# A decoder layer's last stage: seven block products in place of eight, over pairs of 512-token chunks

## The chip, the core and the metric

The kernel runs on one core of a Trainium2 chip. The metric is the device time of one execution in microseconds (us); lower is better. The engines of the core run their own instruction streams side by side: TensorE (PE, matrix products; PEld is its loading of the stationary operand), VectorE (DVE), ScalarE (ACT), GpSimd (POOL) and SyncE (SP, which here issues all transfers). An engine takes its instructions strictly in order and waits at one whose inputs or buffers aren't ready. PE writes its results to PSUM banks, from which DVE and ACT read them; everything else on chip lies in SBUF, 128 partitions wide.

## The reference

One layer for 2048 tokens of width 1024, float32. The stage that changes computes, for a hidden state h that is a scaled and shifted x:

```
u, B, C, g_conv, m_attn, m_conv = h @ W_in columns          (each 1024 wide)
a = (o * silu(g_attn)) @ W_attn_out                         (512 -> 1024)
z = C * u;  y_conv = causal 3-tap convolution of z along tokens + bias
s = (B * y_conv * silu(g_conv)) @ W_conv_out                (1024 -> 1024)
y = (sigmoid(m_attn) * a + sigmoid(m_conv) * s) @ W_o       (1024 -> 1024)
out = LayerNorm(alpha * x + (1 + gate) * y)
```

Ahead of it stands the attention: three dilated groups of heads whose outputs are merged per head with weights from their softmax denominators, and gated, which gives o * silu(g_attn).

## The kernel before

To keep float32 accuracy each operand of a product is split into a rounded high part and the remainder (`split`, L99 and L100: a cast on ACT, then a subtraction on DVE), and a product is three matmuls, high x high, high x low, low x high (L137 to L139). A matmul takes a stationary tile of 128x128 and a moving tile of 128x512.

Stage 1 does two of the attention groups, stage 1b the local group and the merge, stage 2 all the rest. The merge of a head (L561 to L574) loads the weights broadcast from `al_scr` into `ab`, the other groups' outputs into `og`, multiplies and adds on DVE, and stores the result into `om_scr`.

The work of all stages is a list of segments run by `run_segs` (L162): a segment has a weight tile `raw` of 128x1024, whose load is issued five segments ahead and whose split is issued three ahead, and a function that issues its matmuls and what consumes them. Because the list runs across stages and chunks, the preparation of the next chunk and the last merges of stage 1b are issued between matmuls of other work. The order on each engine is then the scheduler's, which sorts by priority in the order of the code and by its estimate of when things are ready.

Stage 2 (L592 to L818) goes through four chunks of 512 tokens. For each chunk it has the eight 128-row tiles of h split (`hhi`, `hlo`), and then, for each of eight column blocks of 128, the projections u, C, g_conv, B (24 matmuls each), with the convolution and the gates on DVE and ACT between them; then for each of eight blocks the two mixes m_attn and m_conv (24 each), the attention output (12) and the convolution output (24), merged into `mg` and split; then the w_o products, token blocks stationary (192 matmuls), and the normalization. One chunk has 1632 matmuls. Nothing of a chunk goes to DRAM but the result. The gate row of the normalization is computed with dots on DVE (L233) during the mixes of the first chunk. The first products of a chunk have the weights stationary and h moving, those with w_o have the merged tokens (`mgh`, `mgl`) stationary and the weights moving (names `hhi`, `whi`).

## Time and profile before

| what | value |
|---|---|
| time, median of three runs | 2704.84 us (2702.08 to 2707.76) |
| the profiled execution's span | 2700.4 us |
| PE busy | 2646.0 us, 98% |
| DVE, ACT, POOL busy | 50%, 32%, 2% |
| moved by DMA | 325.00 MB, mean 120 GB/s |

A row of busy time counts an instruction of an engine from start to end; matmuls overlap each other, so their single durations (some 390 ns) are longer than the distance between two of them. A row of a timeline is the start in us, the duration in us, the engine, the line, the operation and the tiles written and read; what stands in brackets is idle time ahead of it and what ended it. A "granted clock" is the share of PE's full clock that the throttle let it have.

### The profile page before, as it was taken

To read this page: it belongs to the slowest core of one execution; us is meant where nothing else is said; L and a number is where in the kernel's file an instruction comes from. 1 tells how busy PE (TensorE), PEld (TensorE's weight loads), DVE (VectorE), ACT (ScalarE), POOL (GpSimd) and SP (SyncE) were. 2 spreads that over 40 slices of the span, in tenths; PEclk is the share of its full clock that TensorE was granted. 3 is DMA by queue.
4 is the path that set the end of the run, shared out by engine and by line. 5 is a ranking of instruction groups with operands and counts; after the bars stand their busy time and mean duration, and the time that the engine had idled before them with its cause. 6 is when DMAs were issued, how large, how long until landed. Compare 5 with 4: busy or idle time off the path is not lost.

```text
span 2700.4 us, 32783 instructions
## 1 busy us (share of the span) xinstructions
PE 2646.0 (98%) x12910; PEld 2257.3 (84%) x12910; DVE 1346.5 (50%) x2330; ACT 870.3 (32%) x1471; POOL 55.0 (2%) x78
## 2 busy tenths in 40 slices
PE   6999999999999999999999999999999999999998
PEld 4898998989988888887888888888888888888887
DVE  8334334243245765857454564433654434644336
ACT  4233333233333434433232323322232323233221
POOL 2000000000000000000000000000000000000000
PEclk9999999999999999999999999999999999999999
DMA  7223223232233544626233442322432323423222
GB/s 260 82 79 125 82 95 109 75 113 87 74 126 106 186 146 129 204 97 220 102 125 123 147 159 94 113 94 97 160 129 94 117 91 112 163 95 107 96 98 101
DMA packets 141357, 325.00 MB, mean 120 GB/s; under 512 B 18215, under 2 KB 53107, under 8 KB 141204
## 3 DMA queue, kind: packets, MB, share of 16 engines
q1 hardware_dynamic: 141204, 322.92, 35.8%
q8 instruction: 101, 1.65, 0.2%
q14 instruction: 52, 0.43, 0.1%
HBM read 301.58 MB, written 21.28 MB: 120 GB/s over the span
## 4 chain that ended last, share of the span: by engine, by line
PE 88%; DVE 5%; DMA 5%; issue 1%; ACT 0%; SPq 0%; DVEq 0%
PE mm L137 22%; PE mm L138 22%; PE mm L139 22%; PE mm L185 4%; PE mm L184 3%; PE mm L183 3%; DMA og<-o_scr 1%; PE pt L364 1%; DMA xs<-in_xn 1%; DMA ab<-al_scr 1%; DVE hlo L100 1%; PE mm L785 1%; PE mm L783 1%; PE mm L784 1%; PE s L184 1%
## 5 line engine op out<-in xcount | busy, mean ns | idle before, releaser
L137 PE MATMUL mm<-hhi,whi 128*128 128x512 f32 x2392 | 940.3, 393 | 22.2 <-ACT hhi L99 21.4
L138 PE MATMUL mm<-hlo,whi 128*128 128x512 f32 x2392 | 934.1, 391 | 2.2 <-DVE hlo L100 2.2
L139 PE MATMUL mm<-hhi,wlo 128*128 128x512 f32 x2392 | 933.8, 390 | 0.7 <-DVE wlo L100 0.7
L100 DVE TENSOR_TENSOR wlo<-raw,whi 128x1024 fp32r<-128x1024 f32 x423 | 517.4, 1223 | 827.5 <-ACT whi L99 817.5
L99 ACT CAST whi<-raw 128x1024 fp32r<-128x1024 f32 x423 | 444.4, 1051 | 1370.6 <-PE mm L138 598.6
L137 PEld LDWEIGHTS mm<-hhi,whi 128*128 128x128 f32 x2392 | 450.1, 188 | 115.5 <-ACT hhi L99 24.2
L139 PEld LDWEIGHTS mm<-hhi,wlo 128*128 128x128 f32 x2392 | 450.0, 188 | 95.2 <-DVE wlo L100 1.6
L138 PEld LDWEIGHTS mm<-hlo,whi 128*128 128x128 f32 x2392 | 450.4, 188 | 94.4 <-DVE hlo L100 4.1
L183 PE MATMUL mm<-whi,hhi 128*128 128x256 f32 x768 | 246.2, 322 | 3.8 <-ACT hhi L99 3.6
L185 PE MATMUL mm<-whi,hlo 128*128 128x256 f32 x768 | 245.1, 323 | 1.3 <-DVE hlo L100 1.1
L184 PE MATMUL mm<-wlo,hhi 128*128 128x256 f32 x768 | 244.8, 321 | 1.0 <-DVE wlo L100 1.0
L183 PEld LDWEIGHTS mm<-whi,hhi 128*128 128x128 f32 x768 | 182.2, 237 | 7.9 <-ACT hhi L99 6.4
L185 PEld LDWEIGHTS mm<-whi,hlo 128*128 128x128 f32 x768 | 181.4, 237 | 3.9 <-DVE hlo L100 3.2
L184 PEld LDWEIGHTS mm<-wlo,hhi 128*128 128x128 f32 x768 | 181.8, 237 | 1.9 <-DVE wlo L100 1.2
L357 ACT ACTIVATE p<-p,st 128x128 f32<-128x128 f32 (+1 forms) x192 | 86.7, 453 | 71.3 <-DVE st L355 70.8
L137 PE MATMUL mm<-cph,whi 128*128 128x512 f32 x256 | 100.6, 393 | 0.0
L139 PE MATMUL mm<-cph,wlo 128*128 128x512 f32 x256 | 100.2, 392 | 0.0
L138 PE MATMUL mm<-cpl,whi 128*128 128x512 f32 x256 | 99.7, 390 | 0.0
L729 DVE TENSOR_TENSOR sc<-sc,mm 128x512 f32<-128x512 f32 x32 | 22.0, 688 | 123.0 <-PE mm L139 123.0
L99 ACT CAST hhi<-xs 128x512 fp32r<-128x512 f32 x96 | 58.1, 619 | 76.9 <-DVE xs L122 65.4
L122 DVE TENSOR_SCALAR xs<-xs,scp,mod 128x512 f32<-128x512 f32 x96 | 51.4, 543 | 41.0 <-DMA xs<-in_xn 25.4
L100 DVE TENSOR_TENSOR hlo<-xs,hhi 128x512 fp32r<-128x512 f32 x96 | 66.2, 705 | 5.3 <-ACT hhi L99 4.6
(210 smaller groups left out, 2632.0 us busy)
## 6 DMA issues: line engine op xcount, KB each, us to landing
raw<-in_w_main SPq DMA_DIRECT2D x304, 512.0 KB
raw<-in_w_v SPq DMA_DIRECT2D x48, 512.0 KB
xs<-in_xn SPq DMA_DIRECT2D x64, 256.0 KB
raw<-in_w_co SPq DMA_DIRECT2D x32, 512.0 KB
raw<-in_w_o SPq DMA_DIRECT2D x32, 512.0 KB
ab<-al_scr SPq DMA_DIRECT2D x48, 256.0 KB
...
```

The lines of the kernel that those rows point to most:

```text
L99: S.copy(hi, src)
L100: V.tensor_sub(lo, src, hi.bitcast(F32))
L122: E.tensor_scalar(xs, xs, scp[:, k:k + 1], mod[:, 0, k:k + 1], op0=ALU.mult, op1=ALU.add)
L137: PE.matmul(ps, hi[:, sl], xh, start=k == 0, stop=False)
L138: PE.matmul(ps, hi[:, sl], xl, start=False, stop=False)
L139: PE.matmul(ps, lo[:, sl], xh, start=False, stop=k == n - 1)
L183: PE.matmul(o, a[0], b[0], start=start, stop=False)
L184: PE.matmul(o, a[0], b[1], start=False, stop=False)
L185: PE.matmul(o, a[1], b[0], start=False, stop=stop)
L357: S.activation(pt[:, w], pt[:, w], AF.Exp, scale=-1.0, bias=st[:, 0, col:col + 1], accum_out=st[:, 1, col:col + 1])
L364: PE.transpose(ps[:, n * P:(n + 1) * P], P_t[b][:, a:a + P], ident)
L783: PE.matmul(ps, xh[:, ts], hi, start=k == 0, stop=False)
```

## The change

Stage 2 is written anew for two pairs of chunks (1024 tokens each) and in four parts, A to D, each run to its end over all tokens before the next begins. A product of a 2x2 grid of weight blocks and a 2x2 grid of activation blocks takes eight block products; the changed kernel forms seven, from sums and differences of blocks (the Winograd form of Strassen's scheme).

- `t_row` builds for one 128-row of the moving operand the seven combinations: four subtractions and seven splits, into tiles `th` and `tl` of their own for each product and row, one buffer each. For parts A to C the moving operand is h, the gated attention, the gated convolution; for D it is w_o, scaled by the gate row first.
- `stationary_parts` builds for each step the seven combinations of the stationary operand: four sums, three 1024-wide splits (`w2`) and one 512-wide (`w1`).
- `products` issues the seven products in the order 1, 2, 6, 5, 7, 4, 3 into four banks a to d. A bank is copied by ACT (`keep`) and then accumulated onto by the next product; DVE adds a copy and a bank to get each of the four result blocks. `step` issues the loads and stationary parts of a step, and only then (`flush`) the products of the step before.
- Between the parts results go to DRAM and back: `y_scr` (gated convolution), `sg_scr` (the mixes), `pa_scr` (attention output times its mix), `mg_scr` (merged), 42 MB in all.
- The dots of the gate row move from the mixes to part B. In part C, POOL adds the two merged halves, and in part D it adds the LayerNorm's bias; both were on DVE.
- Pools for weights, h and PSUM are now closed with stage 1b, and stage 2 has its own.
- In part D rows are handled 1024 wide, with the normalization on ACT (`Identity` with scale and bias).

```diff
+    y_scr = dram.tile([2, KT, P, 2 * CH], F32, name="y_scr")
+    sg_scr = dram.tile([2, 2, KT, P, 2 * CH], F32, name="sg_scr")
+    pa_scr = dram.tile([2, KT, P, 2 * CH], F32, name="pa_scr")
+    mg_scr = dram.tile([SEQ // P, P, KT, P], F32, name="mg_scr")
...
+    tp = ctx.enter_context(tc.tile_pool(name="tp", bufs=1, reuse_waits="tile"))
+    psum = ctx.enter_context(tc.tile_pool(name="psum2", bufs=1, space=bass.MemoryType.PSUM, reuse_waits="tile"))
...
+    def t_split(T, p, i, src):
+        hi = tp.tile([P, CH], F32R, name=f"th{p}{i}")
+        lo = tp.tile([P, CH], F32R, name=f"tl{p}{i}")
+        split(hi, lo, src)
+        T[p, i] = (hi, lo)
...
+    def t_row(T, i, xa, xb):
+
+        b11, b12, b21, b22 = xa[:, :CH], xa[:, CH:PAIR], xb[:, :CH], xb[:, CH:PAIR]
+        t1, t2, t4 = half(), half(), half()
+        t_split(T, 1, i, b11)
+        t_split(T, 2, i, b21)
+        V.tensor_sub(t1, b12, b11)
+        V.tensor_sub(t2, b22, t1)
+        t_split(T, 6, i, t2)
+        t_split(T, 5, i, t1)
+        V.tensor_sub(b12, b22, b12)
+        t_split(T, 7, i, b12)
+        V.tensor_sub(t4, b21, t2)
+        t_split(T, 4, i, t4)
+        t_split(T, 3, i, b22)
...
+    def stationary_parts(w, raw1, raw2, n):
...
+        a11, a12, a21, a22 = raw1[:, :n], raw1[:, n:2 * n], raw2[:, :n], raw2[:, n:2 * n]
+        one = s_split(w, raw1[:, :2 * n], "w2", 4)
+        put(1, one, 0)
+        put(2, one, 1)
+        x = w.tile([P, 2 * n], F32, name="xs")
+        s1, s2 = x[:, n:], x[:, :n]
+        V.tensor_add(s1, a21, a22)
+        V.tensor_sub(s2, s1, a11)
+        pair = s_split(w, x, "w2", 4)
+        put(6, pair, 0)
+        put(5, pair, 1)
+        V.tensor_sub(a21, a11, a21)
+        pair = s_split(w, raw2[:, :2 * n], "w2", 4)
+        put(7, pair, 0)
+        put(4, pair, 1)
+        s4 = w.tile([P, n], F32, name="s4")
+        V.tensor_sub(s4, a12, s2)
+        put(3, s_split(w, s4, "w1", 1), 0)
+        return S_
...
+    def products(S_, T, rows, c11, c12, c21, c22):
...
+        def prod(bank, p, start):
+            hi, lo = S_[p]
+            for n, i in enumerate(rows):
+                sl = slice(n * P, (n + 1) * P)
+                th, tl = T[p, i]
+                first = start and n == 0
+                kw = dict(skip_group_check=True)
+                PE.matmul(bank, hi[:, sl], th, start=first, stop=False, **kw)
+                PE.matmul(bank, hi[:, sl], tl, start=False, stop=False, **kw)
+                PE.matmul(bank, lo[:, sl], th, start=False, stop=n == len(rows) - 1, **kw)
...
+        a = ps_bank()
+        prod(a, 1, True)
+        r1 = keep(a)
+        b = ps_bank()
+        prod(b, 2, True)
+        c11(r1, b)
+        prod(a, 6, False)
+        r2 = keep(a)
+        c = ps_bank()
+        prod(c, 5, True)
+        prod(a, 7, False)
+        r3 = keep(a)
+        c22(r3, c)
+        d = ps_bank()
+        prod(d, 4, True)
+        c21(r3, d)
+        prod(c, 3, False)
+        c12(r2, c)
...
+    def step(w, src1, src2, n, T, rows, consumer):
+        raws = []
+        for s in ((src1, src2) if src2 is not None else (src1,)):
+            raw = w.tile([P, DM], F32, name="raw", bufs=3)
+            SP.dma_start(raw, s)
+            raws.append(raw)
+        if src2 is None:
+            raws = [raws[0][:, :2 * n], raws[0][:, 2 * n:]]
+        S_ = stationary_parts(w, raws[0], raws[1], n)
+        flush()
+        todo.append(lambda: products(S_, T, rows, *consumer()))
...
+        for p in range(2):
+            T = {}
+            flush()
+            for i in range(4):
+                xa, xb = big(), big()
+                for t, k in ((xa, i), (xb, i + 4)):
+                    for cc in range(2):
+                        SP.dma_start(t[:, cc * CH:(cc + 1) * CH], xn[2 * p + cc, :, k, :])
+                    S.activation(t[:, :PAIR], t[:, :PAIR], AF.Identity, scale=scp[:, k:k + 1],
+                                 bias=mod[:, 0, k:k + 1])
+                t_row(T, i, xa, xb)
...
+                step(w, w_main[W_U + n], w_main[W_C + n], CH, T, range(4), conv)
+                step(w, w_main[W_GC + n], w_main[W_B + n], CH, T, range(4), gates)
...
+                step(w, w_main[W_MA + d], w_main[W_MC + d], CH, T, range(4), mixes)
+        flush()
...
             SP.dma_start(wt, wada[2, k])
-            dot_v(wt, cbox[0], t2("junk")[:, :256], gate_acc)
+            dot_v(wt, cbox[0], half()[:, :256], gate_acc)
             dot_end(2, k, gate_acc)
             V.tensor_scalar_add(mod[:, 2, k:k + 1], mod[:, 2, k:k + 1], 1.0)
...
+        for p in range(2):
+            T = {}
+            rows = range(2 * p, 2 * p + 2)
+            for i in range(2):
+                xa, xb = big(), big()
+                for t, j in ((xa, i), (xb, i + 2)):
+                    for cc in range(2):
+                        SP.dma_start(t[:, cc * CH:(cc + 1) * CH], om_scr[2 * p + cc, :, j, :])
+                t_row(T, 2 * p + i, xa, xb)
...
+                    def gated(k, at):
+                        def f(r, bank):
+                            t = half()
+                            V.tensor_add(t, r, bank)
+                            V.tensor_mul(m[k][:, at:at + CH], m[k][:, at:at + CH], t)
+                            if (k, at) in ((0, CH), (1, 0)):
+                                SP.dma_start(pa_scr[p, d + k], m[k])
+                        return f
+
+                    return gated(0, 0), gated(0, CH), gated(1, 0), gated(1, CH)
+
+                if p == 0:
+                    gate_part(d)
+                    gate_part(d + 1)
+                step(w, w_ao[d // 2], None, 256, T, rows, part)
+        flush()
...
+    with workspace(6, 8) as w:
+        for p in range(2):
+            T = {}
+            flush()
+            for i in range(4):
+                xa, xb = big(), big()
+                for t, k in ((xa, i), (xb, i + 4)):
+                    SP.dma_start(t[:, :PAIR], y_scr[p, k])
+                t_row(T, i, xa, xb)
...
+                    def gated(k, at):
+                        def f(r, bank):
+                            t = half()
+                            V.tensor_add(t, r, bank)
+                            V.tensor_mul(m[k][:, at:at + CH], m[k][:, at:at + CH], t)
+                            G.tensor_add(m[k][:, at:at + CH], m[k][:, at:at + CH], a_[k][:, at:at + CH])
+                            if (k, at) in ((0, CH), (1, 0)):
+                                SP.dma_start(mg_scr[p * 8:(p + 1) * 8, :, d + k, :].rearrange("b q t -> q b t"),
+                                             m[k].rearrange("q (b t) -> q b t", t=P))
+                        return f
+
+                    return gated(0, 0), gated(0, CH), gated(1, 0), gated(1, CH)
+
+                step(w, w_co[d], w_co[d + 1], CH, T, range(4), merged)
+        flush()
...
+    with workspace(5, 6) as w:
+        gate_row = w.tile([P, DM], F32, name="row")
...
+        T = {}
+        for i in range(4):
+            xa, xb = big(), big()
+            for t, k in ((xa, i), (xb, i + 4)):
+                for hh in range(2):
+                    SP.dma_start(t[:, hh * CH:(hh + 1) * CH], w_o[hh, k // 2, :, (k % 2) * CH:(k % 2 + 1) * CH])
+                V.tensor_mul(t[:, :DM], t[:, :DM], gate_row)
+            t_row(T, i, xa, xb)
...
+                def finish(k):
+                    z = zs[k]
+                    V.scalar_tensor_tensor(z, xr[k], ALPHA, z, op0=ALU.mult, op1=ALU.add)
+                    sts = w.tile([P, 2, 6], F32, name="bns", bufs=2)
+                    for hh in range(2):
+                        V.bn_stats(sts[:, hh], z[:, hh * CH:(hh + 1) * CH])
+                    mv = w.tile([P, 2], F32, name="mv", bufs=2)
+                    V.bn_aggr(mv, sts)
+                    V.tensor_scalar_add(mv[:, 1:2], mv[:, 1:2], LN_EPS)
+                    rs = w.tile([P, 2], F32, name="rs", bufs=2)
+                    G.tensor_tensor(rs[:, 0:1], mv[:, 1:2], powe, op=ALU.pow)
+                    V.scalar_tensor_tensor(rs[:, 1:2], mv[:, 0:1], -1.0, rs[:, 0:1], op0=ALU.mult, op1=ALU.mult)
+                    S.activation(z, z, AF.Identity, scale=rs[:, 0:1], bias=rs[:, 1:2])
+                    V.tensor_mul(z, z, lng)
+                    G.tensor_add(z, z, lnb)
+                    SP.dma_start(out[(tb + k) * P:(tb + k + 1) * P, :], z)
+
...
+            step(w, mg_scr[tb].rearrange("q k t -> q (k t)"), mg_scr[tb + 1].rearrange("q k t -> q (k t)"),
+                 CH, T, range(4), norm)
+        flush()
```

Where instructions stand, at three places. First SP, which issues the transfers, at the end of stage 1b. Before, around the start of the last chunk's merge (the weights' store to `al_scr` and their loads into `ab`), with weight loads (`raw`) and hidden-state loads (`xs`) of the next stage:

```order
L118 DMA xs<-in_xn 128x512 x4
L554 DMA al_scr<-al 16x3x128
L104 DMA raw<-in_w_main 128x1024
L561 DMA ab<-al_scr 128x512 x4
L104 DMA raw<-in_w_main 128x1024
L567 DMA og<-o_scr 128x4x128
L104 DMA raw<-in_w_main 128x1024
L561 DMA ab<-al_scr 128x512 x2
L574 DMA om_scr<-o_10073 128x512
L567 DMA og<-o_scr 128x4x128
```

After, from the end of the merge's loads and stores to the first loads of stage 2 (`big<-in_xn`, whose rows T is built from):

```order
L564 DMA ab<-al_scr 128x512
L570 DMA og<-o_scr 128x4x128 x2
L564 DMA ab<-al_scr 128x512
L577 DMA om_scr<-o_10182 128x512
L564 DMA ab<-al_scr 128x512 x2
L570 DMA og<-o_scr 128x4x128 x2
L577 DMA om_scr<-o_10367 128x512
L577 DMA om_scr<-o_10428 128x512
L746 DMA big<-in_xn 128x512 x8
L719 DMA raw<-in_w_main 128x1024 x3
```

The loads for stage 2's first rows stood ahead of the merge's loads before; now they stand behind its last store, and the first weight loads behind those.

Second DVE at the same place: before, the first operations of the last four merges (L564 to L573, on `o`, `ab`, `og`, `gt`) and their neighbours:

```order
L100 TENSOR_TENSOR hlo<-xs,hhi 128x512
L671 SCALAR_TENSOR_TENSOR y<-z,cw,y 128x512
L122 TENSOR_SCALAR xs<-xs,scp,mod 128x512
L564 TENSOR_TENSOR o_10073<-o_10073,ab 128x512
L665 COPY z<-halo 128x2
L569 TENSOR_TENSOR ab<-ab,og 128x4x128
L100 TENSOR_TENSOR wlo<-raw,whi 128x1024
L570 TENSOR_TENSOR o_10073<-o_10073,ab 128x512
L569 TENSOR_TENSOR ab<-ab,og 128x4x128
L572 TENSOR_TENSOR gt_10273<-gt_10273,ab 128x512
```

After, the end of the merges and the start of T's first row (`t` and `tl`):

```order
L573 TENSOR_TENSOR o_10428<-o_10428,ab 128x512
L572 TENSOR_TENSOR ab<-ab,og 128x4x128
L573 TENSOR_TENSOR o_10428<-o_10428,ab 128x512
L576 TENSOR_TENSOR o_10428<-o_10428,gt_10486 128x512
L628 TENSOR_TENSOR t<-big 128x512
L103 TENSOR_TENSOR tl_10603<-big,th_10602 128x512
L629 TENSOR_TENSOR t<-big,t 128x512
L103 TENSOR_TENSOR tl_10617<-t,th_10616 128x512
L103 TENSOR_TENSOR tl_10607<-big,th_10606 128x512
```

and the end of T with the first split of a stationary (`w2l`), without which no product starts:

```order
L103 TENSOR_TENSOR tl_10751<-big,th_10750 128x512
L103 TENSOR_TENSOR tl_10760<-big,th_10759 128x512
L103 TENSOR_TENSOR tl_10756<-t,th_10755 128x512
L103 TENSOR_TENSOR w2l<-raw,w2h 128x1024
L659 TENSOR_TENSOR xs<-xs,raw 128x512
```

The merges stood between operations of stage 2's first projections; now they stand in one piece ahead of all 46 operations of T and the split.

Third DVE between two halves of stage 2. Before, at the first projections of the second chunk, with the normalization (L759 to L774) of the first:

```order
L759 SCALAR_TENSOR_TENSOR cpl<-xh,cpl 128x512
L100 TENSOR_TENSOR wlo<-raw,whi 128x1024
L760 BN_STATS bns_13038<-cpl 128x6
L666 TENSOR_TENSOR z<-mm,u 128x512
L764 BN_AGGR mv<-bns_13038 128x2
L100 TENSOR_TENSOR wlo<-raw,whi 128x1024
L765 TENSOR_SCALAR mv<-mv 128x1
L771 SCALAR_TENSOR_TENSOR cph<-cph,mv,lnrow 128x512
L771 SCALAR_TENSOR_TENSOR cpl<-cpl,mv,lnrow 128x512
```

After, at the start of the second pair of part A, behind the last sums (L810, L814) of the first pair's last step:

```order
L814 TENSOR_TENSOR big<-t,pb 128x512
L103 TENSOR_TENSOR w2l<-raw,w2h 128x1024
L810 TENSOR_TENSOR big<-t,pb 128x512
L628 TENSOR_TENSOR t<-big 128x512
L103 TENSOR_TENSOR w1l<-s_14123,w1h 128x512
L629 TENSOR_TENSOR t<-big,t 128x512
L632 TENSOR_TENSOR big<-big 128x512
L634 TENSOR_TENSOR t<-big,t 128x512
L103 TENSOR_TENSOR tl_13943<-big,th_13942 128x512
L103 TENSOR_TENSOR tl_13947<-big,th_13946 128x512
```

Where a weight split or two stood between the old chunk's last work, now a whole build of T stands behind the last sum, which reads the bank that the old T's last product filled.

## Rows read from the trace of the kernel before

**Rows 1.** The page: span, busy shares, granted clock in 40 slices.

```profile
span 2700.4 us, 32783 instructions
...
PE 2646.0 (98%) x12910; PEld 2257.3 (84%) x12910; DVE 1346.5 (50%) x2330; ACT 870.3 (32%) x1471; POOL 55.0 (2%) x78
...
PEclk9999999999999999999999999999999999999999
```

**Rows 2.** The page: the chain that ended last, by engine.

```profile
PE 88%; DVE 5%; DMA 5%; issue 1%; ACT 0%; SPq 0%; DVEq 0%
```

**Rows 3.** Timeline of DVE and SP at the end of stage 1b.

```profile
1199.39 0.69 DVE L582 COPY gt<-mm 128x512 f32<-128x512 f32 x1 [2.06 <-PE mm L139]
...
1210.54 0.34 SPq L554 DMA_DIRECT2D al_scr<-al  x1
...
1213.37 1.85 SPq L561 DMA_DIRECT2D ab<-al_scr  x4
...
1217.39 0.69 DVE L564 TENSOR_TENSOR o<-o,ab 128x512 f32<-128x512 f32 x1 [0.24 <-DMA ab<-al_scr]
...
1250.01 0.72 DVE L573 TENSOR_TENSOR o<-o,gt 128x512 f32<-128x512 f32 x1
```

**Rows 4.** Timeline: the last matmul and the last DVE operation.

```profile
2691.92 0.28 PE L785 MATMUL mm<-hhi,mgl 128*128 128x256 f32 x1
...
2696.45 0.74 DVE L774 SCALAR_TENSOR_TENSOR xr<-cpl,rs,lnrow 128x512 f32<-128x512 f32 x1
```

**Rows 5.** Stretches: length, PE, PEld, DVE, ACT, POOL busy, clock, DMA share, GB/s.

```profile
1570.00:1890.00 320.00, 320.00 (x1409) 264.51 (x1408) 148.68 (x198) 93.07 (x116) 3.82 (x4) 1.00 0.31 109
1890.00:2210.00 320.00, 320.00 (x1405) 263.81 (x1404) 160.37 (x219) 95.37 (x120) 3.69 (x4) 1.00 0.35 120
```

**Rows 6.** Stretches, PE alone: length, busy, matmuls, clock, DMA share, GB/s.

```profile
1590.00:1750.00 160.00, 160.00 (x708) 1.00 0.33 112
1904.00:1948.00 44.00, 44.00 (x190) 1.00 0.42 140
```

**Rows 7.** Timeline of DVE, back-to-back operations: start, duration.

```profile
1241.26 0.69 DVE L570 TENSOR_TENSOR o<-o,ab 128x512 f32<-128x512 f32 x1
1241.86 0.69 DVE L100 TENSOR_TENSOR cpl<-y,cph 128x512 fp32r<-128x512 f32 x1
...
1244.27 1.22 DVE L100 TENSOR_TENSOR wlo<-raw,whi 128x1024 fp32r<-128x1024 f32 x1
1245.40 1.11 DVE L569 TENSOR_TENSOR ab<-ab,og 128x512 f32<-128x512 f32 x1
```

**Rows 8.** Groups of last stage: count, busy us, mean ns; idle before.

```profile
L99 ACT CAST whi<-raw 128x1024 fp32r<-128x1024 f32 x266 | 279.7, 1052 | 932.1 <-PE mm L138 465.9 <-issue 362.2 <-PE ot L785 54.6
L669 ACT ACTIVATE y<-z,cw 128x512 f32<-128x512 f32 x32 | 26.2, 818 | 12.5 <-DVE z L666 12.5
...
L656 ACT COPY u<-mm 128x512 f32<-128x512 f32 x32 | 18.4, 576 | 0.0
L99 ACT CAST hhi<-xs 128x512 fp32r<-128x512 f32 x28 | 16.6, 620 | 15.9 <-DVE xs L122 15.8
...
L233 DVE CUSTOM_DVE_ANT_0 junk<-raw,xr 128x256 f32<-128x256 f32 x32 | 13.5, 423 | 21.1 <-DMA raw<-in_wada 20.6
...
L233 DVE DVE_READ_ACCUMULATOR2_ANT gate_acc<- 128x1 f32 x32 | 2.6, 83 | 0.0
```

**Rows 9.** The chain in time, end of stage 1b: start, us, what.

```profile
1102.53 6.40 DMA ab<-al_scr
...
1196.67 4.50 DMA xs<-in_xn
```

**Rows 10.** PE after a wait, then that stretch (columns as in Rows 5).

```profile
34.56 0.57 PE L137 MATMUL mm<-hhi,whi 128*128 128x512 f32 x1 [2.98 <-ACT hhi L99]
...
34.50:38.50 4.00, 3.94 (x10) 3.15 (x11) 3.96 (x5) 2.56 (x10) 2.37 (x1) 0.57 0.94 325
```

**Rows 11.** Timeline of POOL, and of DVE beside it.

```profile
22.05 2.51 POOL L277 TENSOR_TENSOR prod<-wt,cb 128x1024 f32<-128x1024 f32 x1 [1.33 <-DMA wt<-in_wada]
...
35.97 2.37 POOL L277 TENSOR_TENSOR prod<-wt,cb 128x1024 f32<-128x1024 f32 x1 [4.28 <-DMA wt<-in_wada]
...
22.27 2.84 DVE L100 TENSOR_TENSOR hlo<-xs,hhi 128x512 fp32r<-128x512 f32 x1
...
35.97 2.65 DVE L233 CUSTOM_DVE_ANT_0 junk<-wt,cb 128x256 f32<-128x256 f32 x1
```

334 lines of the change are left out of this document (136 added, 198 removed).

## The prediction

> **What bounds the kernel now.** I read the page first. TensorE (PE) is busy 98% of a span of 2700.4 us and the clock granted is 9 or more tenths in all forty slices [rows 1]; in the chain that ended last, PE alone is 88% [rows 2]. Then the stretches of the last stage, which begins when the last local gate is copied at 1199.39 [rows 3] and ends with the last matmul at 2691.92 + 0.28 = 2692.2 [rows 4]: 1492.8 us. Within it PE never rests (320.00 of 320.00 us busy) while VectorE (DVE) is busy 148.68 us of them, 46%, ScalarE (ACT) 93.07, 29%, and the DMA engines 31% [rows 5]. So here matmuls are the price and everything else is cover: fewer matmuls are worth their full time as long as the other engines still hide, and each place where they stop hiding is paid in full.
>
> **What is removed.** The last stage issues 6552 matmuls before (1632 for each of four chunks, 24 more since the last block goes in two halves) and 5712 after: a full step is seven products x 4 rows x 3 passes = 84, and there are 48 in part A (24 for each pair of chunks), 8 in part C and 8 in part D, 64 x 84 = 5376; part B has 8 steps of 42, 336. The rate has two values: 160.00 us / 708 = 226.0 ns in the first projections and 44.00 / 190 = 231.6 ns in the w_o stretch [rows 6]. What differs in the built program is where the stationary operand lies: w_o's are above 180 KB of a partition, those of the first projections below 130 KB. The changed kernel puts its stationary tiles at 173 to 221 KB, so I take the w_o row, and keep the other as the low end: 5712 x 0.2316 = 1322.9 us (low 5712 x 0.2260 = 1290.9). A saving of 1492.8 - 1322.9 = 170 us, if PE never waits.
>
> **What is added, and where PE waits for it.** Each of the seven products wants its own moving matrix T. One row of T is seven splits and four subtractions: 11 DVE operations of 128x512, which follow each other every 0.60 us (1241.26 to 1241.86), so 6.6 us; the 1024-wide split takes 1.13 (1244.27 to 1245.40) [rows 7]. ACT's casts beside them, 7 a row at 0.62 or less, are 4.3 us and hide [rows 8]. The T tiles exist once, so a new T can't be written until the last step that reads the old one has passed, and in DVE's order the whole build and the first split of the first stationary (`w2l`) stand behind that step's last consumer. There are six such places:
>
> 1. Into part A. Before, the gated merges of the last local chunk, from 1217.39 to 1250.01 [rows 3], lay under projections of the last stage. Now DVE does all four merges ahead of the first T operation, and SP issues the first load of `in_xn` behind the last `om_scr` store. Behind each merge that waits for `ab` stand all T operations, and behind those PE, which has nothing from 1199.4 on. The statistics still reach `al_scr` at 1210.54 and the loads of `ab` at 1213.37 [rows 3]; without splits between them I let the merges end at 1241 rather than 1250. A load of `in_xn` lands after 4.5 [rows 9], ACT scales the row's two tiles (1.3 us each, an estimate from 0.82 for half the width [rows 8]), so row 0 is ready near 1247.5; 46 operations x 0.60 = 28 and the 1024-wide split at the end bring 1277 to 1278. Wait 79 us (65 if the statistics come sooner and loads overlap the merges; 95 if `ab` and `om_scr` take their 6.4 us in turn [rows 9]).
> 2. Pair 1 of part A: 46 x 0.60 = 27.6 behind the last consumer, plus about 4 for loads that need freed buffers, less some 4 since the first product starts before all seven are built: 28 (20 to 33).
> 3. Part B. It has 336 matmuls, 78 us of PE, but DVE has in it: T 44 x 0.60 = 26, stationaries 8 x 3.4 = 27 (three operations of 0.60 and five half as wide, 0.32 each), consumers 64 x 0.60 = 38, and the dots of the gate row, moved here from under the mixes: 32 x (0.42 + 0.08), with small sums 17 [rows 8]. Sum 108 and 8 for its loads behind the last `sg_scr` stores, 12 for waits between: DVE is the bound, and 108 + 20 - 78 = 50 is lost (35 to 75).
> 4. Part C: loads of `y_scr` behind the `pa_scr` stores on SP, about 7, and 44 x 0.60 + 1.1: 35 (28 to 42).
> 5. Pair 1 of part C: partly interleaved with consumers, 24 (18 to 30).
> 6. Part D: w_o is also scaled by the gate row, two 1024-wide operations a row: 4 x (6.6 + 2.26) = 35.4, the split 1.1, loads 7: 43.5 (36 to 52).
>
> Sum 259.5 (202 to 327). After an idle time PE runs at the lower of the clock's two levels: behind 2.98 us of waiting the window of 4 us had a granted clock of 0.57 [rows 10], that is almost all of it at 1.2 of 2.4 GHz, and costs about 1.7 us. Six restarts: 10.
>
> **Within the steps.** 84 matmuls last 19.5 us. DVE's work in a step by the same 0.60 and 1.13: convolution 13.5, gates 13, mixes 10, part C 11, part D: stationaries 6.4, four sums 2.4, two rows of the normalization 2 x 4 = 8 (two 1024-wide operations of 1.15, two of 0.60, small ones of 0.5), so 17. All fit under 19.5. On SP a step's store waits for its last consumer with the next step's weight loads behind it; those are wanted a step later and need some 6 us (4.5 for half the bytes [rows 9]), so the step hides them, and without that cover each step would lose about those 6. Here a row speaks against the change. Part D gives GpSimd (POOL) the last addition of each row, 128x1024, and part C each merge addition, 128x512. In the trace of before POOL's 1024-wide product at 22.05 runs 2.51 us, and the DVE split that was issued 0.22 us later ran 2.84 instead of 0.69, ending 0.55 after POOL [rows 7, 11]; the same happened at 35.97 [rows 11]. So a POOL operation takes DVE's time too. Two a step make part D's DVE 17 + 2 x 2.6 = 22.2 against 19.5: 8 x 2.7 = 21; I take 19 since a few POOL operations will meet a DVE operation late (0 to 30). In part C four half-wide ones, some 1.3 each (half of POOL's 2.6, an estimate), make 16: still hidden. The Trainium skill, page "SBUF — State Buffer", section "Who interferes with whom", says that a DVE instruction with two SBUF inputs contends with a GpSimd instruction that reads SBUF and that one fully blocks for the other's whole instruction; the trace agrees by those rows. Without such blocking part D would stay hidden and the sum be 19 lower.
>
> **End.** Before, 2700.4 - 2692.2 = 8.2 us follow the last matmul [rows 1, 4]. Now the last block's normalization on 1024-wide rows, with POOL's add at 2.6 and one store of 512 KB, and the second-last row ahead of it: 15 (12 to 18).
>
> **Sum.** 1199.4 + 1322.9 + 259.5 + 10 + 19 + 15 = 2825.8; the median of before, 2704.84, is 4.4 above the profiled span, so 2830. Against before: -170 for matmuls, +296 for waits, end and part D. DMA is no term: it is 31 to 35% busy now at 109 to 120 GB/s [rows 5], and another stretch shows 325 GB/s [rows 10]; the intermediates add 84 MB written and read, and weights read twice or once instead of four times take 76 MB away.
>
> **Rivals.**
> (a) The waits are mostly hidden and the kernel is not slower. Mechanism: T of the next pair or part is built while the closing step's seven products run (19.5 us each), so places 2 to 6 cost nothing and only place 1 stays. Time 2830 - 180.5 - 8.5 = 2641. It decides when all waits with restarts fall under 1492.8 + 8.2 - 1322.9 - 19 - 15 = 144 us, instead of 270 (176 at the faster matmul rate). For it: DVE is under half busy, and first rows of the last product order come free early. Against: single T tiles, which the last step reads to its end, DVE's order, and place 1 with place 3 alone make 129. Chance 0.08; of it a quarter falls within 0.2% of before.
> (b) Worse than forecast: the chain inside a step doesn't fit. After product 7, ACT copies the bank (0.58 [rows 8]), DVE adds it to another bank (0.60), and only then may product 3 write that bank; between them lies product 4, 12 x 0.2316 = 2.8 us. If ACT is in a 1024-wide cast (1.05) and DVE in a 1024-wide split (1.13) or behind POOL (2.6), the chain is 1.05 + 0.58 + 1.13 + 0.60 = 3.4 and with semaphores near 3.8: 1 us in each of 72 steps, 2830 + 70 = 2900. It decides if the scheduler's order puts wide casts just ahead of the copies; as I read ACT's order the casts stand between copies and mostly have their 2.8 us. Chance 0.15.
> (c) That the products aren't seven: excluded, the built program has 5712.
>
> **Chances and range.** Forecast 0.77, (a) 0.08, (b) 0.15. 0.2%, 5 us, is about what a measurement of this kernel can tell from no change. Faster 0.06, same 0.02, slower 0.92. All low ends at once give 1199.4 + 1290.9 + 202 + 10 + 0 + 12 + 4.4 = 2719, all high ones 1199.4 + 1322.9 + 327 + 10 + 30 + 18 + 4.4 = 2912; they won't all fall together, and (b) reaches 2900 with the middle terms. I give 2735 to 2905.
>
> **What would show it.** Six holes in PE between 1199 and the end, the first near 79 us and ending with a DVE split `w2l`; part B with DVE busy throughout and PE about 60%; elsewhere full PE with 231 to 233 ns a matmul (226 would show that place in SBUF was not it, -32 us); in part D, DVE operations of 2.5 us beside POOL's. Wrong would be holes that sum under 150 us, or PE waiting at every step's last product.

## The result and the profile after

The changed kernel takes 2795.05 us (median of four runs, 2793.6 to 2798.35) against 2703.46 for the kernel before, measured beside it (2698.7 to 2707.76): ratio 1.0338, 95% interval 1.0323 to 1.0353. The forecast was 2830 within 2735 to 2905. The profiled execution has a span of 2791.8 us (before 2700.4, [rows 1]). From the page of the changed kernel, the lines that answer to [rows 1]; the last two are PE's busy share and its granted clock in 40 slices of 70 us:

```profile
span 2791.8 us, 31786 instructions
...
PE 2519.3 (90%) x12070; PEld 2115.6 (76%) x12070; DVE 1696.2 (61%) x2816; ACT 1012.5 (36%) x1691; POOL 158.4 (6%) x126
...
PE   6999999999999999927999999899999966787597
...
PEclk9999999999999999968999999999999978899799
```

PE is 127 us less busy and yet the span is 91 us longer: the row of PE shows where, a deep notch in slices 18 and 19 (the entry into part A) and a ragged end (parts B, C and D). Stretches of the parts, columns as in [rows 5]:

```profile
1278.00:1743.00 465.00, 465.00 (x2001) 377.07 (x2000) 291.43 (x365) 164.67 (x200) 0.00 (x0) 1.00 0.24 83
1777.00:2226.00 449.00, 449.00 (x1933) 363.72 (x1932) 274.49 (x345) 156.49 (x191) 0.00 (x0) 1.00 0.22 75
2226.50:2355.20 128.70, 90.65 (x338) 66.97 (x337) 108.27 (x259) 48.28 (x86) 0.00 (x0) 0.83 0.65 233
2620.00:2775.00 155.00, 151.43 (x643) 119.75 (x642) 133.03 (x184) 54.16 (x64) 60.05 (x28) 1.00 0.38 134
```

The two long stretches of part A are full, 465.00 of 465.00 and 449.00 of 449.00: inside them seven products do what they promise. Part B (third line) has PE busy for 90.65 us of 128.70 while DVE works 108.27, and part D (fourth) is nearly full.

The entry into part A, timeline of DVE and of SP's queue, as [rows 3] showed it before:

```profile
1201.89 0.69 DVE L585 COPY gt<-mm 128x512 f32<-128x512 f32 x1 [4.70 <-PE mm L142]
...
1212.42 0.69 DVE L567 TENSOR_TENSOR o<-o,ab 128x512 f32<-128x512 f32 x1 [5.17 <-DMA ab<-al_scr]
...
1238.15 0.69 DVE L576 TENSOR_TENSOR o<-o,gt 128x512 f32<-128x512 f32 x1
1246.19 0.69 DVE L628 TENSOR_TENSOR t<-big 128x512 f32<-128x512 f32 x1 [7.34 <-ACT big L747]
...
1273.95 1.22 DVE L103 TENSOR_TENSOR w2l<-raw,w2h 128x1024 fp32r<-128x1024 f32 x1
...
1239.32 4.20 SPq L746 DMA_DIRECT2D big<-in_xn  x8
```

and PE's first matmuls of part A (brackets: idle time before, and what ended it):

```profile
1256.47 0.80 PE L681 MATMUL pb<-th,w2h 128*128 128x512 f32 x1 [54.62 <-ACT w2h L102]
...
1275.22 0.80 PE L683 MATMUL pb<-th,w2l 128*128 128x512 f32 x1 [16.68 <-DVE w2l L103]
```

Merges until 1238.84, then the first load of `in_xn`, ACT's scaling, 46 operations of T, and last the split `w2l`, which is the third operand that the first step needs. PE had nothing to do from 1201.9 on, but for four matmuls at 1256 to 1258.

The loss of each place is its length less its matmuls times their mean distance in that part (the distance is the time between the starts of two neighbouring matmuls; those of 215 to 262 ns are averaged); a clock restart is in it, as it is in the predicted column.

| place | predicted, us | measured, us |
|---|---|---|
| into A | 79 + 1.7 | 74.1 |
| A, second pair | 28 + 1.7 | 13.7 |
| B | 50 + 1.7 | 50.2 |
| into C | 35 + 1.7 | 36.3 |
| steps of C, first pair | 0 | 5.2 |
| C, second pair | 24 + 1.7 | 12.9 |
| into D | 43.5 + 1.7 | 47.9 |
| steps of D | 19 | 5.6 |
| end, from the last matmul on | 15 | 16 |
| distance of matmuls, all parts | 231.6 ns | A 232.4, B 233.5, C 229.2, D 233.3 ns |

### The profile page after: what moved, and what is told of

Its sections match the earlier page's. It is cut to its first block, busy times and chain, and to the rows that moved or that the text cites. A ratio compares the mean times of both kernels' runs of the same rounds, so it can differ in the third digit from the quotient of the medians.

```text
span 2791.8 us, 31786 instructions
## 1 busy us (share of the span) xinstructions
PE 2519.3 (90%) x12070; PEld 2115.6 (76%) x12070; DVE 1696.2 (61%) x2816; ACT 1012.5 (36%) x1691; POOL 158.4 (6%) x126
## 5 line engine op out<-in xcount | busy, mean ns | idle before, releaser
L681 PE MATMUL pb<-th,w2h 128*128 128x512 f32 x1632 | 653.3, 402 | 144.7 <-ACT w2h L102 122.7
L683 PE MATMUL pb<-th,w2l 128*128 128x512 f32 x1632 | 648.0, 399 | 55.9 <-DVE w2l L103 55.9
L682 PE MATMUL pb<-tl,w2h 128*128 128x512 f32 x1632 | 650.9, 400 | 2.5 <-DVE tl L103 2.5
L681 PEld LDWEIGHTS pb<-th,w2h 128*128 128x128 f32 x1632 | 312.1, 191 | 229.2 <-ACT w2h L102 127.3
L103 DVE TENSOR_TENSOR wlo<-raw,whi 128x1024 fp32r<-128x1024 f32 x155 | 189.6, 1223 | 419.8 <-ACT whi L102 412.9
L683 PEld LDWEIGHTS pb<-th,w2l 128*128 128x128 f32 x1632 | 312.0, 191 | 132.6 <-DVE w2l L103 59.9
L682 PEld LDWEIGHTS pb<-tl,w2h 128*128 128x128 f32 x1632 | 312.5, 192 | 76.7 <-DVE tl L103 4.3
L140 PE MATMUL mm<-hhi,whi 128*128 128x512 f32 x856 | 341.9, 399 | 22.0 <-ACT hhi L102 22.0
L142 PE MATMUL mm<-hhi,wlo 128*128 128x512 f32 x856 | 335.9, 392 | 3.1 <-DVE wlo L103 3.1
L141 PE MATMUL mm<-hlo,whi 128*128 128x512 f32 x856 | 335.5, 392 | 1.7 <-DVE hlo L103 1.7
```

Source lines behind the costliest of these rows:

```text
L103: V.tensor_sub(lo, src, hi.bitcast(F32))
L140: PE.matmul(ps, hi[:, sl], xh, start=k == 0, stop=False)
L141: PE.matmul(ps, hi[:, sl], xl, start=False, stop=False)
L142: PE.matmul(ps, lo[:, sl], xh, start=False, stop=k == n - 1)
L681: PE.matmul(bank, hi[:, sl], th, start=first, stop=False, **kw)
L682: PE.matmul(bank, hi[:, sl], tl, start=False, stop=False, **kw)
```

## Experiments

The theory was that of the prediction: six places where PE waits for DVE, plus a lock between POOL and DVE in part D, plus a slower spacing of matmuls because the stationary operands lie high in SBUF. The rivals for the first were hidden preparation and a chain inside each step; for the last, see the later runs.

**1. The first step's stationary parts ahead of T.** `step` can prepare and hold; A, C and D call it so before the loop that builds T:

```diff
+            ahead = []
+            step(w, w_main[W_U], w_main[W_C], CH, T, range(4), None, hold=ahead)
             for i in range(4):
                 xa, xb = big(), big()
...
-                step(w, w_main[W_U + n], w_main[W_C + n], CH, T, range(4), conv)
+                step(w, w_main[W_U + n], w_main[W_C + n], CH, T, range(4), conv, ready=ahead)
```

> The stationary parts of the first step of a moving matrix T are loaded and split before T is built (part A both pairs, part C both pairs, part D); nothing else is changed. Theory: most of the loss at the entries of A, C and D is not T itself but the first stationary split, which stands behind all of T on DVE, so that matmuls can't follow T's rows as they are made. At the second pair of A that split was early and the loss is 13.9 us instead of 28 or more. Expected: the second holes (17.3 us into A, 11.6 into C, 25.5 into D) shrink to 0 to 3, the first grow by about 3 (split ahead of T), total 35 to 50 us less, time about 2750. Rival: DVE's sum of operations sets when the step ends, and moving one operation only moves the hole: under 12 us less, time above 2783.

Measured 2754.84 us (ratio 1.0194, 1.0173 to 1.0215), the number expected, for a reason that was not. The second hole at each entry is gone, but the products then follow T row by row, so the entries still lose 59.7 (A), 27.8 (C) and 37.1 us (D). Later steps give much of that back, part D's above all, which lose 14.7 instead of 5.6: by the starts of the matmuls A loses 12.5 us less, C 2.5 and D 1.2, some 16 us in all. The rest, some 27 us, came out of the matmuls: 226.7 ns apart in A where they had been 232.4. (The last stage began 2.4 us later.) The stationary tiles had moved from 173 to 141 KB by the order of allocation, which fitted the theory on height.

**2. The last chunk's merge left out.**

```diff
+            if c == NCH - 1:
+                SP.dma_start(om_scr[c, :, j, :], o0[j])
+                return
```

> The gated merge of the last local chunk is left out: its heads are stored unmerged and ungated. Theory: the hole of 72 us ahead of part A is a sum in order, 37 us of merges (from 1201.9 to 1238.8), 7.4 us of loads behind the last store, 28 us of T and the first split. Without merges the loads can start near 1203, and the hole shrinks by 33 to 38 us; time about 2760. Rival: T's tiles or the loads wait for something else of the stage before (freed space, statistics), and the hole stays above 55 us.

Measured 2769.08 us, span 2765.9. DVE's first T operation stands at 1214.83 instead of 1246.19, and of the first wait 22.6 us are left of 54.6; groups of PE in this run from 1200 to 1262, the idle time before them last:

```profile
L684 PE MATMUL pb<-th,w2h 128*128 128x512 f32 x23 | 10.4, 452 | 22.6 <-ACT w2h L102 22.6
...
L686 PE MATMUL pb<-th,w2l 128*128 128x512 f32 x22 | 9.5, 440 | 16.6 <-DVE w2l L103 16.6
```

32 us, about what the merges and the wait for `ab` ahead of them took ([rows 3] have them under other work). The second hole (16.6) is T's own. The time, 26 us less, is 9 above the expected 2760: the hole shrank by 32 and not 33 to 38, the last stage began 2 us later, and the matmuls of A are 232.8 ns apart instead of 232.4, some 2 us more.

**3. The gate row's dots moved from part B into part A's second pair**, one for each `mixes` step:

```diff
                 step(w, w_main[W_MA + d], w_main[W_MC + d], CH, T, range(4), mixes)
+                if p == 1:
+                    gate_part(d)
...
-                if p == 0:
-                    gate_part(d)
-                    gate_part(d + 1)
```

> The dots of the gate row (32 of 0.42 us and small sums, 17 us of DVE) move from part B to the second pair's mixes in part A, where DVE is about half busy. Theory of the prediction: part B is bound by DVE's sum (108 us of work against 78 of matmuls), so B gets 13 to 17 us shorter, from 128.7 to about 113, A keeps its 19.5 us a step, time about 2779. Rival: B is held by the order (the second pair's T behind the first pair's steps, the loads at its start), the dots lie in DVE's waits anyway: B shrinks by less than 5 us.

Measured 2780.44 us; part B went from 128.7 to 111.3 us, and part A stayed full. That is the 17 us that the prediction counted for the dots, but DVE's busy time in B fell by 14 (108.27 to 94.32 from 2231.3 to 2342.7); the other 3 are waits that went with it. PE's largest wait in part B, of the changed kernel and then of this run:

```profile
L681 PE MATMUL pb<-th,w2h 128*128 128x512 f32 x96 | 41.9, 443 | 33.9 <-ACT w2h L102 24.7 <-ACT t L687 9.0
```

```profile
L681 PE MATMUL pb<-th,w2h 128*128 128x512 f32 x96 | 39.9, 421 | 21.4 <-ACT w2h L102 16.8 <-ACT t L687 4.6
```

The releaser named is ACT, but what shrank is DVE's work: ACT's casts wait for sums that DVE makes (12.5 us for `xs` in the changed kernel). So DVE's work sets B's length, as far as these 17 us show it; the dots' eight loads left B with it, and what those alone were worth was not tried.

**4. POOL's additions given back to DVE.**

```diff
-                            G.tensor_add(m[k][:, at:at + CH], m[k][:, at:at + CH], a_[k][:, at:at + CH])
+                            V.tensor_add(m[k][:, at:at + CH], m[k][:, at:at + CH], a_[k][:, at:at + CH])
...
-                    G.tensor_add(z, z, lnb)
+                    V.tensor_add(z, z, lnb)
```

> The additions that POOL does in parts C (32 of 128x512) and D (16 of 128x1024) are done by DVE. Theory from the trace after: in part D PE waits 0.8 us a step ahead of product 3 because the sum that must read the bank first stands behind a 1024-wide split on DVE, not because POOL blocks DVE (a sum that reads one operand from PSUM ran 0.64 us beside POOL). So the waits of 0.6 to 1.1 us a step in D stay, D keeps 163 us within 5 (DVE has 2.3 us more a step, in its free time), and the end behind the last matmul shrinks by 1 to 3 us; time 2790 to 2800. Rival, as in the prediction: POOL's lock is what costs in D; then the waits go, D shrinks by 6 to 8 us.

Measured 2788.4 us, 6.6 less, though DVE has more to do: my expectation, that the waits of D stay, was wrong, and they went as the rival, POOL's lock, had it. Groups of DVE in part D (2615 to 2776) of the changed kernel, with POOL's own group last:

```profile
L931 DVE SCALAR_TENSOR_TENSOR big<-big 128x1024 f32<-128x1024 f32 x15 | 23.5, 1570 | 0.3
L948 DVE TENSOR_TENSOR big<-t,pb 128x512 f32<-128x512 f32 x31 | 20.4, 675 | 5.4 <-ACT t L687 3.0 <-PE pb L683 2.5
...
L658 DVE TENSOR_TENSOR xs<-raw 128x512 f32<-128x512 f32 x7 | 15.3, 2179 | 0.0
...
L943 POOL TENSOR_TENSOR big<-big,row 128x1024 f32<-128x1024 f32 x14 | 44.7, 3189 | 42.0 <-DVE big L942 19.7 <-issue 16.2 <-DVE mv L936 3.2
```

and of DVE in this run:

```profile
L948 DVE TENSOR_TENSOR big<-t,pb 128x512 f32<-128x512 f32 x32 | 21.7, 677 | 5.6 <-PE pb L683 2.9 <-ACT t L687 2.7
L931 DVE SCALAR_TENSOR_TENSOR big<-big 128x1024 f32<-128x1024 f32 x16 | 19.5, 1222 | 0.3
...
L658 DVE TENSOR_TENSOR xs<-raw 128x512 f32<-128x512 f32 x8 | 5.4, 680 | 0.0
```

Two operations with both inputs in SBUF are stretched beside POOL, L658 from 680 to 2179 ns and L931 from 1222 to 1570. The sum L948, one of whose inputs is a PSUM bank, is not: 675 and 677. The lock thus cost DVE 7 x 1.5 + 15 x 0.35 = 15.7 us. PE, which lost 5.6 us in the steps of D, is full there in this run (columns as in [rows 6]):

```profile
2620.00:2770.00 150.00, 149.95 (x641) 1.00 0.42 142
```

This run takes more than the lock away, though: POOL's `rs` (L939) no longer stands behind an addition on POOL, and DVE's order is another (a split now ahead of L942). That POOL's additions cost PE these 5.6 us is shown, by which of these ways is not.

**5. The stationary tiles low, T behind them.** A pool of their own ahead of `tp` puts them at 17 to 53 KB.

```diff
+    sp = ctx.enter_context(tc.tile_pool(name="sp", bufs=1, reuse_waits="tile"))
...
-        hi = w.tile([P, n], F32R, name=tag + "h", bufs=bufs)
-        lo = w.tile([P, n], F32R, name=tag + "l", bufs=bufs)
+        full = DM if tag == "w2" else CH
+        hi = sp.tile([P, full], F32R, name=tag + "h", bufs=bufs)[:, :n]
+        lo = sp.tile([P, full], F32R, name=tag + "l", bufs=bufs)[:, :n]
...
-    with workspace(7, 8) as w:
+    with workspace(7, 5) as w:
```

> The changed kernel with the stationary tiles (w2, w1) in a pool of their own below T: 17 to 53 KB of a partition instead of 173 to 213; T moves up to 53 to 165 KB; part B has 5 buffers of 128x512 instead of 8. Theory of the prediction: the distance between matmuls follows where the stationary lies, high ones are the slow ones. In the first experiment the stationaries of part A had come to lie at 141 to 183 KB by another order of allocation, and its matmuls ran at 226.7 ns instead of 232.4, which was most of its gain. Expected here: A, C and D at 226 to 228 ns, some 30 us less, time 2762 to 2772. Rival: the rate comes from the phase between matmuls that the start of a part sets, or from T above 128 KB; then 231 to 234 ns stay in A and D, time above 2785.

Measured 2775.39 us: 226.7 ns in A, 228.8 in B, 226.7 to 227.4 in C and D, holes as before, the steps of D waiting more (up to 1.19 us each, where it was up to 0.69). A little above the expectation, and no decision yet between height and something else that moved with it.

**6. As 1, but in part A row 0 of T is built first**, so that the allocation order puts A's stationary tiles back at 173 KB:

```diff
             for i in range(4):
                 xa, xb = big(), big()
+                if i == 1:
+                    step(w, w_main[W_U], w_main[W_C], CH, T, range(4), None, hold=ahead)
```

> As the first experiment, but in part A the first row of T is built before the first step's stationary parts, by which the buffers are allocated in the old order and the stationaries of A lie again at 173 to 213 KB; C and D as in the first experiment. Theory (place of the stationary): A's matmuls are back at 232 to 233 ns, C and D at 227 to 228; A is 22 to 27 us longer than in the first experiment, the hole into A is shorter by 3 to 7; time 2770 to 2780. Rival (order or phase): A stays at 226.7 ns and the time is about 2750.

Measured 2786.06 us. A's matmuls are back at 232.4 ns, those of C and D, whose tiles stay at 141 KB, at 227. So the place seemed to do it and not the order of the step; the time is some 6 us above what I expected, of which a start that is 3 to 5 us later is the larger part.

**7. Eight products in the same structure**: T has four splits a row and no subtraction, a step's stationary parts are two splits, and a bank takes two products with nothing kept:

```diff
-        prod(a, 1, True)
-        r1 = keep(a)
...
-        prod(c, 3, False)
-        c12(r2, c)
+        for p, q, put_out in ((1, 1, c11), (3, 3, c22), (3, 1, c21), (1, 3, c12)):
+            bank = ps_bank()
+            prod(bank, p, q, True)
+            prod(bank, p + 1, q + 1, False)
+            put_out(None, bank)
```

> The four parts, the steps and the intermediates via DRAM stay, but with the plain eight block products: T has four splits a row and no subtraction, the stationary parts are two splits, results are copied from a bank that holds both products. 6528 matmuls instead of 5712. Its stationaries lie at 109 to 137 KB. Theory: the loss is one of the structure, holes where a part starts, and of T's and the stationaries' DVE work; the seven products save their 816 matmuls. At 226.7 ns 6528 matmuls are 1480 us; the holes shrink with T's build from 244 to about 155 (62 into A, 8, 25 in B, 25, 5, 30); time 2830 to 2880, slower than the changed kernel by 35 to 85. Rival: the work for the seven products costs more than they save, then this is faster than the changed kernel, under 2795.

Measured 2857.6 us (2854.45 to 2860.75). Inside this structure seven products are therefore worth 62.5 us; it is the structure, chunks in pairs with one T and parts run one behind the other, that costs more than that: with eight products it takes 151 us more than the kernel before, not all of it in waits (its end is 8 us longer, and its matmuls are further apart than those of the kernel before, see run 9). It loses 118 us too: 41.5 into A, 21.4 in B, 22.5 into C, 28 into D, and next to nothing at the second pairs. PE's groups from 1201 to 1243 show the same two waits, shorter:

```profile
L657 PE MATMUL pb<-th,w2h 128*128 128x512 f32 x2 | 1.4, 712 | 16.1 <-ACT w2h L102 16.1
L659 PE MATMUL pb<-th,w2l 128*128 128x512 f32 x1 | 0.8, 793 | 23.3 <-DVE w2l L103 23.3
```

And one number that the theory on height can't have: in part A the matmuls are 232.4 ns apart, with the stationary tiles at 109 to 137 KB, lower than in run 1 where they were 226.7.

**8. Runs 1, 3 and 4 together.**

> The first, third and fourth experiments together: first stationary split ahead of T (with the stationaries at 141 to 185 KB), gate dots in part A, additions on DVE. Theory: the gains lie at different places and add up: 2755 from the first, 14 to 17 less in part B, 7 to 12 less in D with the end: 2725 to 2738, still slower than before by about 1%. Rival: DVE in D, with the additions and the early split, becomes the bound, and the time stays above 2745.

Measured 2718.23 us (2713.85 to 2720.23), ratio 1.0045 (1.0028 to 1.0063): better than expected and still slower than before. It is 76.8 us below the changed kernel, where the three gains add up to 61.5; part of the difference is that the steps of D wait 4.7 us here and 14.7 in run 1, where POOL had its additions. Its page:

```profile
span 2714.7 us, 31744 instructions
...
PE 2508.9 (92%) x12070; PEld 2115.1 (78%) x12070; DVE 1700.7 (63%) x2864; ACT 1011.4 (37%) x1691; POOL 53.3 (2%) x78
```

Its places lose 60 (into A), 15 (second pair), 30.5 (B), 28.6 and 15 (C), 37.3 and 4.7 (D), with the rest 196 us; (6552 - 5712) x 0.2267 = 190 are saved. So the last stage takes 1496.9 us to its last matmul where it took 1492.8; it begins 4.2 us later, and the end is 6 us longer: the 14.3 us between the spans.

**9. What sets the distance.** With the addresses that the built programs give their tiles, the matmuls of 128x512 in the last stage fall into classes by one number, the address of the moving operand less that of the stationary one, modulo 256 bytes:

| difference, bytes | mean distance, ns | where (matmuls) |
|---|---|---|
| 0 | 226.7 to 227.0; run 6: 227.6 | before: all but w_o and the attention output (5362); run 1: A, C, D; run 5: all; run 6: C, D |
| 64 | 228.9 to 230.3 | before: attention output (383); after: C (619); run 7: C (754) |
| 128 | 232.4; runs 2 to 4: 232.8 to 232.9 | after: A (3984); run 7: A (4591); runs 2 to 4: A |
| 32, 96, 192 | 233.3 to 233.5 | before: w_o (744); after: B (273), D (643); run 7: B (374), D (753) |

T lies at 96 modulo 256 in the changed kernel; the tile `big`, 8 bytes wider than 4096, shifts what is allocated behind it. A part in which PE waits often has a higher mean: B in run 5 has 228.8 ns at a difference of 0, with a median of 227. This was read out of the traces at hand, so it needed a test of its own. The changed kernel with a pad of 32 to 128 bytes in front of each part's tiles (`n_big` counts the `big` tiles):

```diff
+            if n_big % 8:
+                w.tile([P, 64 - 8 * n_big % 64], F32, name="pad")
```

> The changed kernel with one unused tile of 32 to 128 bytes at the start of each part's workspace, so that every stationary of parts A to D lies a whole multiple of 256 bytes from the moving block sums that it is used with; every engine's order is as in the changed kernel, the stationaries stay within 128 bytes of where they were (173 to 213 KB up). Theory (the spacing of 128x512 matmuls goes by the difference of the two operands' addresses modulo 256 bytes): 226.7 ns in every part in place of 232.4 (A), 233.2 (B), 229.0 (C) and 233.3 (D); by 4032, 336, 672 and 672 matmuls that is 23 + 2 + 1.6 + 4.4 = 31 us, some of D's given back because its steps then wait longer for VectorE: 2764 to 2770 us. Rival 1 (the spacing goes by how high the stationaries lie): nothing moves, 2795 us. Rival 2 (the spacing goes by what order or phase the steps have): nothing moves, 2795 us. The holes stay as they are by all three.

Measured 2770.41 us (2767.14 to 2774.87; ratio 1.0237, 1.0223 to 1.0251), 24.6 less than the changed kernel and at the upper end of what the theory gave. PE alone in the two pairs of part A (length, busy, matmuls, clock, DMA share, GB/s), first of the changed kernel, then of run 7, then of this run:

```profile
1320.00:1700.00 380.00, 380.00 (x1637) 1.00 0.23 79
1820.00:2180.00 360.00, 360.00 (x1551) 1.00 0.23 79
```

```profile
1320.00:1700.00 380.00, 380.00 (x1637) 1.00 0.20 68
```

```profile
1320.00:1700.00 380.00, 380.00 (x1679) 1.00 0.24 83
1820.00:2180.00 360.00, 360.00 (x1590) 1.00 0.23 80
```

380 / 1637 = 232.1 ns and 380 / 1679 = 226.3, at a clock of 1.00 in all, with the stationary tiles at 173 to 213 KB in both kernels. Nothing but addresses differs, by less than 256 bytes: both rivals fall. Of the 31 us that the matmuls are shorter by, part B gives its 2 back at once (129.7 us against 128.7) and part D most of its 4.4 (its steps wait 8.9 us instead of 5.6).

**10. The same in the kernel before.** There 744 recorded matmuls of the merged projection and 383 of the attention output have a difference. One tile is allocated wider than it is used:

```diff
-                z = p_t.tile([P, CH + 2], F32, name="z", bufs=2)
+                z = p_t.tile([P, CH + 64], F32, name="z", bufs=2)[:, :CH + 2]
```

> The kernel before, with its tile z allocated 64 columns wider than used, so that the tiles behind it (og, the attention output that moves, and mg, the merged weight that stands) lie a whole multiple of 256 bytes from their partners; every engine's order is as before. Theory (difference of the operands' addresses modulo 256 bytes): the 768 matmuls of the merged projection go from 233.3 to 226.7 ns and 384 of the attention output from 230.3 to 227 ns, 5.1 + 1.3 = 6.4 us less: 2697 to 2699 us where the kernel before has 2704 to 2706. Rival (height or order): no change within 1 us.

Measured 2696.1 us (2690.64 to 2697.86) against 2706.1 of the kernel before, measured beside it: ratio 0.9956, interval 0.9943 to 0.997. It beats both kernels. The two stretches of [rows 6] in this run:

```profile
1590.00:1750.00 160.00, 160.00 (x707) 1.00 0.34 111
1904.00:1948.00 44.00, 44.00 (x196) 1.00 0.46 146
```

707 matmuls where there were 708, as it should be where nothing differs, and 196 in the w_o stretch where there were 190: 224.5 ns by this count and 226.7 by the distances. From the same instruction to the last matmul, first in the kernel before (its last matmul is in [rows 4]), then in this one:

```profile
1251.38 0.50 PE L137 MATMUL mm<-hhi,whi 128*128 128x512 f32 x1 [0.57 <-DVE sg L678]
```

```profile
1254.86 0.50 PE L137 MATMUL mm<-hhi,whi 128*128 128x512 f32 x1 [0.72 <-DVE sg L678]
...
2687.51 0.28 PE L785 MATMUL mm<-hhi,mgl 128*128 128x256 f32 x1
```

2691.92 - 1251.38 = 1440.5 and 2687.51 - 1254.86 = 1432.7, 7.9 us less for 6.4 expected. The other 1.5 us are in the convolution output, whose 768 matmuls have a difference of 0 in both kernels. Before, they follow the attention output (64) in each block, and the first ten are 224 to 236 ns apart in the mean, 226.7 only from the eleventh on; all together 228.7. In this run all are at 226.7. So a difference slows down some of the matmuls behind it as well, and the 0 row of the table hides these in its 227.0.

## Why the prediction was right, and where it was not

The span came out at 2791.8 for a sum of 2825.8. By the prediction's own terms:

- **Matmuls** (1322.9): 5712 at the distances of the table make some 1326. The value was right and its premise was wrong. Height in SBUF seemed to part the two rates of [rows 6], and it does not: run 7 is slow at 109 KB, run 9 fast at 173 to 213 KB. The w_o stretch of before was slow because of its operands' difference of 192 bytes, the changed kernel because of others. That the forecast's 231.6 ns came true is thus luck; another order of allocation made it 226.7 in run 1, and the prediction allowed for that only as its low end. Both its rates, counted in a short stretch, are a little low: by their starts the matmuls of [rows 6] are 226.7 and 233.3 ns apart.
- **Place 1**, into A (79 + 1.7): 74.1. Merges to 1238.84 (forecast 1241), T from 1246.19 (1247.5), matmuls from 1275.22 (1277 to 1278): the chain was followed step by step, and run 2 took its first link away, with 32 us.
- **Place 2** (28 + 1.7): 13.7, the largest miss among the holes. The step that failed is that the whole build and the split stand behind the last consumer. In the timeline of DVE that split comes 21 us ahead of the last consumer (L810 at 1744.62); the one that "The change" lists between the last sums, at 1742.72, is already the second step's:

```profile
1723.20 1.23 DVE L103 TENSOR_TENSOR w2l<-raw,w2h 128x1024 fp32r<-128x1024 f32 x1 [0.20 <-ACT w2h L102]
...
1744.62 0.69 DVE L810 TENSOR_TENSOR big<-t,pb 128x512 f32<-128x512 f32 x1 [0.67 <-PE pb L683]
1745.32 0.69 DVE L628 TENSOR_TENSOR t<-big 128x512 f32<-128x512 f32 x1
```

  PE begins at 1748.94 and goes through rows of several products as they are finished: 81 matmuls between 1744 and 1777 while T is built. The prediction counted that overlap as 4 us; it is some 18. Place 5 is the same in smaller (12.9 for 25.7).
- **Steps of C** (nothing): 5.2, in the third and fourth step of the first pair. The prediction had the step hide its weight loads and DVE's 16 us of work. Here DVE, in its order, waited for a weight load, and the sum that product 3 needs stood behind it; the next nine matmuls are 0.41 to 0.43 us apart at a granted clock of 0.55 (2449.1 to 2452.9), mostly the lower level, and the wait costs 4.1 us with them:

```profile
2446.48 0.69 DVE L658 TENSOR_TENSOR xs<-raw 128x512 f32<-128x512 f32 x1 [2.88 <-DMA raw<-in_w_co]
...
2449.15 0.61 PE L681 MATMUL pb<-th,w1h 128*128 128x512 f32 x1 [2.22 <-DVE t L888]
```

- **Place 3**, part B (50 + 1.7): 50.2, by the mechanism named: DVE 108.27 us busy for a forecast of 108, and run 3 takes out what it holds of foreign work. The loss isn't spread over the part as a plain sum of DVE's work would have it: 31.7 us lie at the first step, while T is built, 5.8 and 10.3 at the third and fourth, and 1.1 or less at each other step.
- **Places 4 and 6** (36.7 and 45.2): 36.3 and 47.9. Into D, PE's groups from 2565 to 2620 show the two waits, for the first cast and then for the split at the end of T:

```profile
L681 PE MATMUL pb<-th,w2h 128*128 128x512 f32 x10 | 5.3, 529 | 19.9 <-ACT w2h L102 19.9
...
L683 PE MATMUL pb<-th,w2l 128*128 128x512 f32 x9 | 4.3, 498 | 24.9 <-DVE w2l L103 24.9
```

- **Steps of D** (19): 5.6. That POOL's additions cost time there was right (run 4), the size was not: the forecast charged DVE 2.6 us for each of two POOL additions a step, 42 us in all, where the lock costs it 15.7, since the sums that read a PSUM bank don't meet it. The charge was above its own rows, too: in [rows 11] the split loses 2.84 - 0.69 = 2.15 us. With 15.7 us over eight steps DVE's 17 would have been 19.0, inside the step of 19.5 us, and the term near nothing. What is left shows in one step, DVE, ACT, POOL and PE:

```profile
2663.26 2.78 DVE L658 TENSOR_TENSOR xs<-raw 128x512 f32<-128x512 f32 x1
...
2665.45 0.99 POOL L939 TENSOR_TENSOR rs<-mv,powe 128x1 f32<-128x1 f32 x1
...
2666.67 1.25 ACT L941 ACTIVATE big<-big,rs 128x1024 f32<-128x1024 f32 x1 [4.17 <-DVE rs L940]
...
2667.82 1.03 ACT L102 CAST w2h<-raw 128x1024 fp32r<-128x1024 f32 x1
...
2668.76 0.57 ACT L687 COPY t<-pb 128x512 f32<-128x512 f32 x1
...
2669.09 1.22 DVE L103 TENSOR_TENSOR w2l<-raw,w2h 128x1024 fp32r<-128x1024 f32 x1
...
2669.25 3.30 POOL L943 TENSOR_TENSOR big<-big,row 128x1024 f32<-128x1024 f32 x1 [2.81 <-DVE big L942]
...
2670.23 1.28 DVE L948 TENSOR_TENSOR big<-t,pb 128x512 f32<-128x512 f32 x2
...
2670.96 0.50 PE L681 MATMUL pb<-th,w1h 128*128 128x512 f32 x1 [0.69 <-DVE big L948]
```

  An addition on POOL (L943) runs from 2662.15 to 2665.48 and holds back both DVE's sum L658 and POOL's own `rs`. So ACT comes late to the scaling L941, and the copy of the bank stands behind that and a cast. The rest is rival (b) in little: the copy is done at 2669.33, DVE is in a 1024-wide split until 2670.31, and product 3 waits 0.69 us. In part A, 48 steps of it, nothing of the kind is seen (full stretches), so (b) as a whole fell; the sign of being wrong that the prediction named, PE waiting at the last product, shows in six steps of part D with 0.22 to 0.69 us and twice in part C. The Trainium skill, page "SBUF — State Buffer", section "Who interferes with whom", has the distinction that the prediction passed over: a DVE instruction with at most one SBUF input, outside the modes that use two ports, does not contend with GpSimd. The rows of L948 (675 and 677 ns) and L658 (2179 and 680) agree.
- **Rival (a)**, hidden waits, would have needed T to be built under the closing step. At places 1, 3, 4 and 6 PE waited nearly as long as forecast, so that did not happen there; whether single T tiles or DVE's order stood against it, as the prediction held, no run parted.
- **End** (15): 16, with the same lock once more: of the last two rows, one's scaling on DVE (L942) takes 3.32 us beside the other's addition on POOL (L943, 2.34 us), where it takes 1.22 in the mean of part D.

Together: holes and restarts 269.5 became 235.1 (-34), C's steps +5, D's steps -13, start +2, matmuls and remainders +5, end +1: 2825.8 - 34 = 2791.8.
